# Ties in the gates, key tiles 0 and 1 turned into one tile's two banks, and the last SwiGLU block's two last products exchanged

## The chip, the cores and the metric

The kernel runs on one core of one Trainium2 chip. The metric is the device time of one execution in microseconds (us). A core has five engines with instruction queues of their own: TensorE (PE in the profile, with its weight loads as PEld), VectorE (DVE), ScalarE (ACT), GpSimd (POOL) and SyncE (SP, used here to issue transfers). Each works through its own queue in order and waits for the others by semaphores. An instruction that waits holds up everything behind it in its own queue.

## The reference

One encoder layer over 16 learned meta tokens and 512 tokens, width 1024, in float32:

```python
xn = rmsnorm(h, norm_mix_g)
sb_q, sb_k, sb_v, df_q, df_k, df_v = split(xn @ w_in)
o_sb = stick-breaking attention(sb_q, sb_k, sb_v)            # 8 heads of 128
o_df = differential attention(df_q, df_k, df_v)              # 8 heads, two softmax maps of 64
o_df = rmsnorm(o_df, subln_g) * (1 - lam_init)               # per head
y_sb = o_sb @ w_br_sb
y_df = o_df @ w_br_df
gates = sigmoid(xn @ w_gate + b_gate)                        # two gates of 1024 channels
h = h + (gates[0] * y_sb + gates[1] * y_df) @ w_out
hn = rmsnorm(h, norm_ffn_g)
h = h + (silu(hn @ w_ffn_gate) * (hn @ w_ffn_up)) @ w_ffn_down   # inner width 2816
y = rmsnorm(h, norm_final_g)
```

## The kernel before, in words

Every float32 product is made of three TensorE products of a rounded high half and a low remainder. `split` makes the halves of a weight tile: a ScalarE cast (`wh`, line 78) and a VectorE subtraction (`wl`, line 79). `mm3` (lines 290 to 292) issues the three products, and the third is the one that needs `wl`. The weights arrive in chunks of 512 KB through SP (line 204), are staged, split some chunks ahead of use (`prepare`), and used once. Several large products (keys and values of most heads, the output projection, the SwiGLU block) are made of seven block products instead of eight, from sums of blocks; `c1` to `c4` prepare the weight sums.

The order of the work is only partly written by hand. The program is traced in order, and a planner puts every instruction into its engine's queue: of those that are ready by its own estimate, it takes the one that was traced first. `tc.high_priority(offset=EVAC)` moves an instruction ahead in that ranking, `tc.add_manual_dep` ties an instruction behind another one. The planner's durations are estimates, so the order that it fixes may be wrong for the chip.

The stages that the change touches, in order of time:

- **Attention heads** (eight stick-breaking heads, then eight differential ones). In each, `attn_out` turns the attention blocks (query by key) into key by query with TensorE transposes (line 555), key tile by key tile j = 0, 1, 2. Tile 0 has four blocks (512 columns), tile 1 three, tile 2 two, and one more block (line 557) makes `a_f`. ScalarE copies each turned tile from PSUM as `a_h` (line 559), VectorE makes the remainder `a_l` (line 560), and `weighted` multiplies them with the values (lines 290 to 292, 582, 583). `turn_first` does tiles 0 and 1, `turn_rest` does tile 2. PSUM has eight banks of 512 columns: the pool `ps_z` has two tiles of two banks each (`z_tile`), the pool `ps_mm` four tiles of one bank (`mm_tile`, `tr_tile`). A stick-breaking head takes two z tiles for its turn: tile 0 goes into bank 0 of the first, tile 1 into bank 0 of the second, tile 2 into bank 1 of the first. A differential head takes single banks of `ps_mm`.
- **End of the last differential head.** Its norm (`norm`, lines 769 to 776: Ln and Exp on ScalarE with a VectorE step between it and `o_h`, then `o_l`) is run late, among the gate products. The gates of channel blocks f = 1 and 2 are copied out raw (line 807), and their four sigmoids (line 1053) follow in the trace after all that. Sigmoid is in another function table of ScalarE than Ln and Exp; a change of table is an instruction of its own in the profile (ACT_TABLE_LOAD).
- **Gates and merge** (lines 1105 to 1128). For f in the order 1, 2, 0, 3 to 7: the branch outputs `y_sb` and `y_df`, which were summed up in DRAM, are loaded (line 1065, into memory that the attention pool held before), multiplied by the gates (line 1122: on GpSimd for f < 6, on VectorE after), and added (the merge, line 1126); `merge_sums` splits the result for the output projection. The gates for f = 0 were stored early and come back by a load with a sigmoid behind it (lines 1117, 1118). The last y outputs are added up in DRAM by transfers that GpSimd issues (line 800). Then the residual input is loaded into `hres` by four transfers that GpSimd issues (line 1133); the output projection adds to it (line 1207).
- **SwiGLU block**, 22 blocks f of 128 channels, each in seven block products with `first`, `second`, `third`. `third` ends a block with product a22 into bank e1 and product s4 into bank e3; `second` has copied e1 as `qx` and `qy` (lines 1317, 1322) and added e3 to `qy` (line 1323). The last block is followed by the down projection, whose first weight chunks go into the memory of `hT_l` (the tile `slots`).

Of the kernel before, what the change touches and what calls it, by code (L numbers as in the profile page):

```python
# [41 lines left out]
def block_kernel(ctx: ExitStack, tc: tile.TileContext, x, meta, norm_mix_g, w_in, w_gate, b_gate,  # L42
# [33 lines left out]

    def split(hi, lo, src, lo_eng=None, hi_copy=None):
        cast["last"] = (hi_copy or nc.scalar.copy)(hi, src)  # L78
        (lo_eng or nc.vector).tensor_tensor(lo, src, hi.bitcast(F32), op=ALU.subtract)  # L79

    stream = []

# [133 lines left out]
    def generic(n):  # L216
        wh, wl = parts(n)
        split(wh, wl, staged[n], nc.gpsimd if n < 3 else None)

    K1, K2 = slice(0, 4), slice(4, 8)  # L220

# [9 lines left out]
    def c2(f, g, u, pool, bufs):  # L231
        s = pool.tile([P, KT, P], F32, tag="s21", bufs=bufs, name="s21")
        first = nc.vector.tensor_tensor(s[:, K2], u[:, K1], u[:, K2], op=ALU.add)
        if f in (2, 3):
            behind = mybir.DependencyInfo(mybir.DependencyClass.Sync, mybir.DependencyReason.DATA)
            tc.add_manual_dep(first.ins, cast["hn" if f == 2 else "bf"].ins.name, behind)
        nc.vector.tensor_tensor(s[:, K1], s[:, K2], g[:, K1], op=ALU.add)
        wh, wl = chunk()
        split(wh, wl, s)
        ops[f, "s2"], ops[f, "s1"] = (wh[:, K1], wl[:, K1]), (wh[:, K2], wl[:, K2])  # L240
        ops[f, "s"] = s
# [302 lines left out]
    def attn_out(blocks, d, lo_rows, banks):  # L544

        qn = P - lo_rows
        off = (0, 512, 896)
        a_h = ap_.tile([P, 1152], F32R, tag="a_h", name="a_h")
        a_l = ap_.tile([P, 1152], F32R, tag="a_l", name="a_l")
        a_f = ap_.tile([P, P], F32, tag="a_f", name="a_f")  # L550

        def turn(j, pt):
            n = 512 - j * P
            for t in range(j, NQ):
                nc.tensor.transpose(pt[:, (t - j) * P:(t - j + 1) * P], blocks(t, j * P, (j + 1) * P), ident)  # L555
            if j == 2:
                nc.tensor.transpose(pt[:, 384:512], blocks(3, 3 * P, 4 * P), ident)
            c = slice(off[j], off[j] + n)
            nc.scalar.copy(a_h[:, c], pt[:, 0:n])
            nc.vector.tensor_tensor(a_l[:, c], pt[:, 0:n], a_h[:, c].bitcast(F32), op=ALU.subtract)  # L560

        def turn_first():
            for j, pt in enumerate(banks(2)):
                turn(j, pt)
            for t in range(NQ):
                b = blocks(t, (t + 1) * P - 32 + NM, (t + 1) * P + NM)
                for i in range(qn // 32):
                    nc.vector.transpose(a_s[32 * t:32 * t + 32, t * qn + 32 * i:t * qn + 32 * i + 32],
                                        b[lo_rows + 32 * i:lo_rows + 32 * i + 32])

        def turn_rest():
            p2 = banks(1)[0]
            turn(2, p2)
            nc.scalar.copy(a_f, p2[:, 384:512])

        def weighted():
            vf, vh, vl = d["v"]
            ps = z_tile()[:, 0]
            for j in range(3):
                n = 512 - j * P  # L580
                mm3(ps[:, j * P:512], [(vh[:, j], vl[:, j], a_h[:, off[j]:off[j] + n], a_l[:, off[j]:off[j] + n])], j == 0, False)
            nc.tensor.matmul(ps[:, 3 * P:512], lhsT=vf[:, 0], rhs=a_f, start=False, stop=False)
            nc.tensor.matmul(ps.rearrange("p (t q) -> p t q", q=P)[:, :, lo_rows:P], lhsT=vf[:, 1],
                             rhs=a_s[:, 0:4 * qn], start=False, stop=True)
            return ps

        return turn_first, turn_rest, weighted


# [20 lines left out]
    def sb_head(h, d, o_h, o_l):  # L610
        qh, ql = d["q"]
        kh, kl = d["k"]
        zA, zB = z_tile(), z_tile()

        def score(o, t, k0, k1):
            q = slice(t * P, (t + 1) * P)
            mm3(o, [(qh[:, q], ql[:, q], kh[:, k0:k1], kl[:, k0:k1])])

        score(zA[:, 0, 0:256], 0, 0, 256)
        score(zA[:, 0, 144:416], 1, 0, 272)  # L620
        score(zA[:, 1, 0:416], 2, 0, 416)
        score(zB[:, 0, 0:HL], 3, 0, HL)
        score(zB[:, 1, 0:HL], 3, HL, L)
        res = []
        for z, n in ((zA, 416), (zB, HL)):
            zz = z[:, :, 0:n]
            e = ap_.tile([P, 2, n], F32, tag=("w2" if n == 416 else "w1"), name="e")
            s = ap_.tile([P, 2, n], F32, tag=("w3" if n == 416 else "w0"), name="s")
            nc.scalar.activation(e, zz, AF.Abs)
            nc.scalar.activation(e, e, AF.Exp, scale=-1.0)  # L630
            nc.scalar.activation(e, e, AF.Ln, bias=1.0)
            nc.vector.scalar_tensor_tensor(s, zz, 0.0, e, op0=ALU.max, op1=ALU.add)  # L632
            sf = s.rearrange("p a b -> p (a b)")
            for a, b in (((0, 144), (144, 416), (416, 816)) if n == 416 else ((0, L),)):
                f = sf[:, a:b][:, ::-1]
                nc.vector.tensor_tensor_scan(f, resets[:, L - (b - a):][:, ::-1], f, BIG, op0=ALU.mult, op1=ALU.add)  # L636
            nc.vector.tensor_tensor(s, zz, s, op=ALU.subtract)  # L637
            nc.scalar.activation(s, s, AF.Exp)
            res.append(sf)
        base = ((0, 0), (0, 144), (0, 416), (1, 0))  # L640
        zs = []

        def banks(n):
            if n == 1:
                return [zs[0][:, 1]]
            zs.extend((z_tile(), z_tile()))
            return [z[:, 0] for z in zs]

        t1, t2, av = attn_out(lambda t, k0, k1: res[base[t][0]][:, base[t][1] + k0:base[t][1] + k1], d, 96, banks)
        yield 4 if h + 1 < SEVEN else 5  # L650
        t1()
        yield 1
        t2()
        yield 1
        ps = av()
        nc.scalar.copy(o_h, ps)
        nc.vector.tensor_tensor(o_l, ps, o_h.bitcast(F32), op=ALU.subtract)
# [36 lines left out]
    def df_head(h, d, o_h, o_l):  # L694
# [72 lines left out]
        def norm():  # L767
            pv = tr_tile()
            nc.tensor.matmul(pv, lhsT=ones_r, rhs=sql, start=True, stop=False)
            nc.tensor.matmul(pv, lhsT=ones_r, rhs=sqh, start=False, stop=True)  # L770
            nc.scalar.activation(sq, pv, AF.Ln, bias=eps_c)
            nc.scalar.activation(sq, sq, AF.Exp, scale=-0.5)
            nc.vector.scalar_tensor_tensor(sq, pv, var_max, sq, op0=ALU.is_le, op1=ALU.mult)
            nc.vector.tensor_tensor(of, of, sq, op=ALU.mult)
            nc.scalar.activation(o_h, of, AF.Copy, scale=g_sub)
            nc.vector.scalar_tensor_tensor(o_l, of, g_sub, o_h.bitcast(F32), op0=ALU.mult, op1=ALU.subtract)  # L776
# [273 lines left out]
        for u in units:  # L1050
            u()
    for sg in sg0 + sg1:
        nc.scalar.activation(sg, sg, AF.Sigmoid)
    att.close()


# [54 lines left out]
    for i, f in enumerate(merge_order):  # L1111
# [3 lines left out]
        for br, y in enumerate(ys[i]):  # L1115
            if f == 0:
                nc.sync.dma_start(sg[br], g_part[br])
                nc.scalar.activation(sg[br], sg[br], AF.Sigmoid)
            elif f > 2:
                for u in gate(br, f, sg[br], AF.Sigmoid):  # L1120
                    u()
            (nc.gpsimd if f < 6 else nc.vector).tensor_tensor(sg[br], sg[br], y, op=ALU.mult)
        if f == KT - 1:
            prepare(prep_at["out", "s1", 2])
        m = mf[:, f] if f < 4 else sg[0]
        nc.vector.tensor_tensor(m, sg[0], sg[1], op=ALU.add)
        merge_sums(f, m)
    use_table(LN_EXP)


    hres = xtp.tile([P, NQ, D], F32, tag="y_sb", name="hres")
    for t in range(NQ):
        nc.gpsimd.dma_start(hres[:, t], xv[:, t])
    ssq = [small.tile([P, 2], F32, tag=f"ssq{t}", bufs=2, name="ssq") for t in range(NQ)]

    hT_h, hT_l = (xtp.tile([P, NM + KT * SEQ], F32R, tag=t, name=n)[:, NM:].rearrange("p (k t) -> p k t", t=SEQ)
# [134 lines left out]
    with tc.tile_pool(name="ffn", bufs=1) as fp:  # L1271
# [53 lines left out]

        def third(f, qx, qy):
            e1, e2, e3, sg = bank[f]
            product(f, "a22", tsum["t4"], e1, False)
            with tc.high_priority(offset=EVAC):
                nc.vector.scalar_tensor_tensor(aT[:, f, T1], e1, -1.0, sg[:, T1], op0=ALU.mult, op1=ALU.mult)  # L1330
            product(f, "s4", tsum["b22"], e3, False)
            with tc.high_priority(offset=EVAC):
                nc.vector.tensor_tensor(sg[:, T2], e3, qx, op=ALU.add)
            nc.scalar.activation(sg[:, T2], sg[:, T2], AF.Silu)
            nc.vector.scalar_tensor_tensor(aT[:, f, T2], qy, -1.0, sg[:, T2], op0=ALU.mult, op1=ALU.mult)

        for f in range(2):
            sg = fw.tile([P, SEQ], F32, tag="sg", bufs=2, name="sg")
# [191 lines left out]
```

## Time and profile before

| | |
|---|---|
| times of three runs | 950.56, 948.53 and 2375.36 us, median 950.56 |
| the profiled execution's own time | 949.31 us |
| its span in the profile | 947.5 us |
| TensorE busy | 929.5 us of the span |
| VectorE, ScalarE, GpSimd busy | 733.9, 586.3, 186.8 us |
| mean granted TensorE clock | 0.997 |
| transfers | 158.41 MB |

The profile is of one execution. Its times count from the start of the span. A row of the timeline has the start, the duration, the engine, the line of the kernel, the operation, the tile written and the tiles read (`out<-in`), the shape, and in brackets how long the engine had stood idle and what ended that. A row of the waits has the waiting engine and line, the releaser, the total in us, the number and the longest. A row of the windows has the stretch, its length, busy time (and count) of PE, PEld, DVE, ACT and POOL, the granted clock, the busy share of the DMA engines and GB/s.

### The profile page before, as it was taken

How to read it: one execution, taken by the hardware profiler on the slowest of the kernel's cores; microseconds unless marked ns; L12 is line 12 of the kernel's file. 1: busy time of each engine (PE TensorE's matmuls, PEld its weight loads, DVE VectorE, ACT ScalarE, POOL GpSimd, SP SyncE). 2: the span in 40 equal slices, each digit the busy share in tenths (PEclk: the TensorE clock that was granted, in tenths of full speed). 3: DMA queues.
4: the chain of work that ended last, by engine and by line, in shares of the span. 5: the costliest groups of instructions: out<-in, count | busy, mean ns of one | idle time of the engine just before them, and what ended most of it. 6: DMA issues, size and time to landing. Idle time of an engine off the chain costs nothing.

```text
span 947.5 us, 16049 instructions
## 1 busy us (share of the span) xinstructions
PE 929.5 (98%) x6009; PEld 843.6 (89%) x6010; DVE 733.9 (77%) x1400; ACT 586.3 (62%) x1105; POOL 186.8 (20%) x211
## 2 busy tenths in 40 slices
PE   8999999999999999999999899999999999999997
PEld 5988999898999999999887688899999999978886
DVE  6988878776678766787653578899888888989875
ACT  6665676676656666666774355765555555566654
POOL 3000121222323344344504330001000000000013
PEclk9999999999999999999999999999999999999999
DMA  8525778778767889799958854537743343286642
GB/s 248 143 68 157 176 170 203 168 164 251 192 198 184 196 190 190 162 208 191 198 155 203 262 172 163 144 80 175 158 124 112 93 131 90 68 259 202 198 153 89
DMA packets 155823, 158.41 MB, mean 167 GB/s; under 512 B 6465, under 2 KB 117218, under 8 KB 155746
## 3 DMA queue, kind: packets, MB, share of 16 engines
q1 hardware_dynamic: 132690, 101.61, 35.9%
q0 software_dynamic: 22896, 55.72, 28.8%
q8 instruction: 47, 0.77, 0.3%
q14 instruction: 30, 0.25, 0.1%
q10 hardware_dynamic: 160, 0.07, 0.0%
HBM read 133.64 MB, written 50.86 MB: 195 GB/s over the span
## 4 chain that ended last, share of the span: by engine, by line
PE 76%; DVE 12%; issue 4%; ACT 3%; DMA 3%; POOL 1%; SPq 0%; POOLq 0%; ACTq 0%; DVEq 0%
PE mm L292 17%; PE mm L291 17%; PE mm L290 17%; PE z L290 6%; PE z L291 6%; PE z L292 6%; DVE wl L79 3%; DVE s L636 2%; PE z L705 1%; PE z L704 1%; ACT wh L78 1%; PE tr L555 1%; DMA wsu<-in_w_in_dram 1%; DVE s L637 1%; DVE s L632 1%
## 5 line engine op out<-in xcount | busy, mean ns | idle before, releaser
L292 PE MATMUL mm<-xT_h,wl 128*128 128x264 f32 (+2 forms) x656 | 213.5, 325 | 3.3 <-DVE wl L79 3.3
L291 PE MATMUL mm<-xT_l,wh 128*128 128x264 f32 (+2 forms) x656 | 214.3, 327 | 0.5
L290 PE MATMUL mm<-xT_h,wh 128*128 128x264 f32 (+2 forms) x656 | 214.3, 327 | 0.5 <-ACT xT_h L909 0.5
L79 DVE TENSOR_TENSOR wl<-wst,wh 128x1024 fp32r<-128x1024 f32 (+1 forms) x147 | 166.4, 1136 | 31.1 <-ACT wh L78 30.7
L78 ACT CAST wh<-wst 128x1024 fp32r<-128x1024 f32 (+1 forms) x147 | 141.8, 966 | 76.2 <-PE mm L291 55.2
L292 PEld LDWEIGHTS mm<-xT_h,wl 128*128 128x128 f32 x656 | 124.0, 189 | 13.7 <-DVE wl L79 3.7
L290 PEld LDWEIGHTS mm<-xT_h,wh 128*128 128x128 f32 x656 | 124.0, 189 | 10.4 <-ACT xT_h L909 0.9
L291 PEld LDWEIGHTS mm<-xT_l,wh 128*128 128x128 f32 x656 | 123.8, 189 | 10.4 <-DVE xT_l L910 1.3
L290 PE MATMUL mm<-hT_h,wh 128*128 128x256 f32 x304 | 85.9, 284 | 1.2 <-ACT qx L1317 0.8
L292 PE MATMUL mm<-hT_h,wl 128*128 128x256 f32 x304 | 85.9, 284 | 0.0
L291 PE MATMUL mm<-hT_l,wh 128*128 128x256 f32 x304 | 85.8, 283 | 0.0
L290 PEld LDWEIGHTS mm<-hT_h,wh 128*128 128x128 f32 x304 | 57.9, 191 | 1.8 <-ACT qx L1317 1.2
L292 PEld LDWEIGHTS mm<-hT_h,wl 128*128 128x128 f32 x304 | 58.1, 191 | 0.0
L291 PEld LDWEIGHTS mm<-hT_l,wh 128*128 128x128 f32 x304 | 58.1, 191 | 0.0
L708 DVE CUSTOM_DVE_ANT_0 pr<-z,bias 128x144 f32<-128x144 f32 (+3 forms) x64 | 30.9, 501 | 34.2 <-PE z L705 31.9
L290 PE MATMUL mm<-o_h,wh 128*128 128x512 f32 x128 | 53.2, 415 | 0.1
L291 PE MATMUL z<-wl,da 128*128 128x512 f32 (+1 forms) x132 | 50.4, 382 | 0.6 <-DVE wl L79 0.6
L291 PE MATMUL mm<-o_l,wh 128*128 128x512 f32 x128 | 50.1, 391 | 0.3 <-DVE o_l L776 0.3
L290 PE MATMUL z<-wh,da 128*128 128x512 f32 (+1 forms) x132 | 50.3, 381 | 0.0
L1432 POOL TENSOR_TENSOR outs<-hres,gF 128x512 f32<-128x512 f32 x4 | 6.2, 1548 | 223.6 <-DVE hres L1418 216.8
L292 PE MATMUL z<-wh,da 128*128 128x512 f32 (+1 forms) x132 | 50.2, 380 | 0.0
L292 PE MATMUL mm<-o_h,wl 128*128 128x512 f32 x128 | 50.2, 392 | 0.0
(366 smaller groups left out, 2515.5 us busy)
## 6 DMA issues: line engine op xcount, KB each, us to landing
wst<-in_w_in_dram SPq DMA_DIRECT2D x40, 512.0 KB, 5.9
ds<-in_w_ffn_down_dram POOLq DMA_DIRECT2D x30, 512.0 KB, 6.1
wst<-in_w_ffn_gate_dram SPq DMA_DIRECT2D x22, 512.0 KB, 4.0
wsu<-in_w_ffn_up_dram SPq DMA_DIRECT2D x20, 512.0 KB, 3.8
wst<-in_w_gate_dram SPq DMA_DIRECT2D x16, 512.0 KB, 8.6
y_df<-y_out POOLq DMA_DIRECT2D x32, 256.0 KB, 7.2
slots<-ds SPq DMA_DIRECT2D x13, 512.0 KB, 3.3
os<-in_w_out_dram POOLq DMA_DIRECT2D x12, 512.0 KB, 4.6
```

Of the source, the lines that this page charges most:

```text
L78: cast["last"] = (hi_copy or nc.scalar.copy)(hi, src)
L79: (lo_eng or nc.vector).tensor_tensor(lo, src, hi.bitcast(F32), op=ALU.subtract)
L290: nc.tensor.matmul(ps, lhsT=ah, rhs=bh, start=(start and i == 0), stop=False, skip_group_check=skip)
L291: nc.tensor.matmul(ps, lhsT=ah, rhs=bl, start=False, stop=False, skip_group_check=skip)
L292: nc.tensor.matmul(ps, lhsT=al, rhs=bh, start=False, stop=(stop and i == n - 1), skip_group_check=skip)
L555: nc.tensor.transpose(pt[:, (t - j) * P:(t - j + 1) * P], blocks(t, j * P, (j + 1) * P), ident)
L632: nc.vector.scalar_tensor_tensor(s, zz, 0.0, e, op0=ALU.max, op1=ALU.add)
L636: nc.vector.tensor_tensor_scan(f, resets[:, L - (b - a):][:, ::-1], f, BIG, op0=ALU.mult, op1=ALU.add)
L637: nc.vector.tensor_tensor(s, zz, s, op=ALU.subtract)
L704: nc.tensor.matmul(o, lhsT=q[c][:, qs], rhs=k[c][:, 0, k0:k1], start=True, stop=False)
L705: nc.tensor.matmul(o, lhsT=q[c][:, qs], rhs=k[c][:, 1, k0:k1], start=False, stop=True)
L708: nc.vector.tensor_tensor_reduce(po, zz, bb, scale=1.0, scalar=-3.0e38, op0=ALU.add, op1=ALU.max, accum_out=mx[:, t, c:c + 1])
```

## The change

- `split` also remembers its subtraction, and `generic` the subtraction of the last weight chunk split (`cast["split"]`). A helper `behind` makes the tie that `c2` wrote out before.
- In the heads, both transposes of `turn_first` are traced ahead of both copies. A stick-breaking head takes one z tile for key tiles 0 and 1 (its two banks) and another one for key tile 2.
- The four sigmoids at line 1053 are tied behind the last norm's Exp (`cast["norm"]`).
- For f = 3 to 6, the merge is tied behind the last weight split traced before it.
- The four loads of `hres` are tied behind the last GpSimd multiply (`cast["gated"]`, f = 5).
- In the last SwiGLU block, `third` traces product s4 and what follows it ahead of product a22 and what follows that.

```diff
     def split(hi, lo, src, lo_eng=None, hi_copy=None):
         cast["last"] = (hi_copy or nc.scalar.copy)(hi, src)
-        (lo_eng or nc.vector).tensor_tensor(lo, src, hi.bitcast(F32), op=ALU.subtract)
+        cast["lo"] = (lo_eng or nc.vector).tensor_tensor(lo, src, hi.bitcast(F32), op=ALU.subtract)
+
+    def behind(ins, name):
+        tc.add_manual_dep(ins.ins, cast[name].ins.name,
+                          mybir.DependencyInfo(mybir.DependencyClass.Sync, mybir.DependencyReason.DATA))
...
         split(wh, wl, staged[n], nc.gpsimd if n < 3 else None)
+        cast["split"] = cast["lo"]
...
         def turn(j, pt):
-            n = 512 - j * P
             for t in range(j, NQ):
                 nc.tensor.transpose(pt[:, (t - j) * P:(t - j + 1) * P], blocks(t, j * P, (j + 1) * P), ident)
-            if j == 2:
-                nc.tensor.transpose(pt[:, 384:512], blocks(3, 3 * P, 4 * P), ident)
+
+        def keep(j, pt):
+            n = 512 - j * P
             c = slice(off[j], off[j] + n)
             nc.scalar.copy(a_h[:, c], pt[:, 0:n])
             nc.vector.tensor_tensor(a_l[:, c], pt[:, 0:n], a_h[:, c].bitcast(F32), op=ALU.subtract)
 
         def turn_first():
-            for j, pt in enumerate(banks(2)):
-                turn(j, pt)
+            both = banks(2)
+            for j in range(2):
+                turn(j, both[j])
+            for j in range(2):
+                keep(j, both[j])
...
         def turn_rest():
             p2 = banks(1)[0]
             turn(2, p2)
+            nc.tensor.transpose(p2[:, 384:512], blocks(3, 3 * P, 4 * P), ident)
+            keep(2, p2)
             nc.scalar.copy(a_f, p2[:, 384:512])
...
-        zs = []
-
-        def banks(n):
-            if n == 1:
-                return [zs[0][:, 1]]
-            zs.extend((z_tile(), z_tile()))
-            return [z[:, 0] for z in zs]
-
-        t1, t2, av = attn_out(lambda t, k0, k1: res[base[t][0]][:, base[t][1] + k0:base[t][1] + k1], d, 96, banks)
+        t1, t2, av = attn_out(lambda t, k0, k1: res[base[t][0]][:, base[t][1] + k0:base[t][1] + k1], d, 96,
+                              lambda n: (lambda z: [z[:, i] for i in range(n)])(z_tile()))
...
-            nc.scalar.activation(sq, sq, AF.Exp, scale=-0.5)
+            cast["norm"] = nc.scalar.activation(sq, sq, AF.Exp, scale=-0.5)
...
     for sg in sg0 + sg1:
-        nc.scalar.activation(sg, sg, AF.Sigmoid)
+        behind(nc.scalar.activation(sg, sg, AF.Sigmoid), "norm")
...
-            (nc.gpsimd if f < 6 else nc.vector).tensor_tensor(sg[br], sg[br], y, op=ALU.mult)
+            if f < 6:
+                cast["gated"] = nc.gpsimd.tensor_tensor(sg[br], sg[br], y, op=ALU.mult)
+            else:
+                nc.vector.tensor_tensor(sg[br], sg[br], y, op=ALU.mult)
...
-        nc.vector.tensor_tensor(m, sg[0], sg[1], op=ALU.add)
+        merged = nc.vector.tensor_tensor(m, sg[0], sg[1], op=ALU.add)
+        if 2 < f < KT - 1:
+            behind(merged, "split")
         merge_sums(f, m)
...
     for t in range(NQ):
-        nc.gpsimd.dma_start(hres[:, t], xv[:, t])
+        behind(nc.gpsimd.dma_start(hres[:, t], xv[:, t]), "gated")
...
+            def up():
+                product(f, "a22", tsum["t4"], e1, False)
...
+            def gate_and_up():
+                product(f, "s4", tsum["b22"], e3, False)
...
+            for half in (up, gate_and_up) if f < NFF - 1 else (gate_and_up, up):
+                half()
```

More of the change, by code (lines that the diff above doesn't have):

```diff
@@ L234, in c2 @@
         if f in (2, 3):
-            behind = mybir.DependencyInfo(mybir.DependencyClass.Sync, mybir.DependencyReason.DATA)
-            tc.add_manual_dep(first.ins, cast["hn" if f == 2 else "bf"].ins.name, behind)
+            behind(first, "hn" if f == 2 else "bf")
         nc.vector.tensor_tensor(s[:, K1], s[:, K2], g[:, K1], op=ALU.add)
@@ L1327, in third @@
             e1, e2, e3, sg = bank[f]
[L1328 to L1335, printed above, removed]
+            def up():
+                product(f, "a22", tsum["t4"], e1, False)
+                with tc.high_priority(offset=EVAC):
+                    nc.vector.scalar_tensor_tensor(aT[:, f, T1], e1, -1.0, sg[:, T1], op0=ALU.mult, op1=ALU.mult)
+            def gate_and_up():
+                product(f, "s4", tsum["b22"], e3, False)
+                with tc.high_priority(offset=EVAC):
+                    nc.vector.tensor_tensor(sg[:, T2], e3, qx, op=ALU.add)
+                nc.scalar.activation(sg[:, T2], sg[:, T2], AF.Silu)
+                nc.vector.scalar_tensor_tensor(aT[:, f, T2], qy, -1.0, sg[:, T2], op0=ALU.mult, op1=ALU.mult)
+            for half in (up, gate_and_up) if f < NFF - 1 else (gate_and_up, up):
+                half()
         for f in range(2):
```

## The prediction

> **What bounds the kernel now.** I read the busy times first, then TensorE's (PE's) waits, and then went to each wait with the timeline.
>
> ```profile
> PE 929.5 (98%) x6009; PEld 843.6 (89%) x6010; DVE 733.9 (77%) x1400; ACT 586.3 (62%) x1105; POOL 186.8 (20%) x211
> ...
> PE mm L292 <- DVE wl L79: 3.3, 1, 3.3
> PE z L555 <- DVE a_l L560: 1.5, 2, 1.0
> ...
> 525.00:540.00 15.00, 11.70 (x44) 8.95 (x43) 7.19 (x7) 5.42 (x9) 7.00 (x8) 0.89 0.85 264
> 540.00:815.00 275.00, 274.59 (x2056) 262.12 (x2055) 235.30 (x374) 160.51 (x270) 14.54 (x12) 1.00 0.48 133
> 940.00:948.00 8.00, 0.64 (x6) 0.44 (x4) 2.11 (x8) 2.34 (x6) 0.72 (x1) 0.84 0.34 131
> ```
>
> PE is busy for 929.5 of 947.5 us, so only 18 us are idle, and 7.4 of them are the last stretch, where nothing is left to multiply. No edit adds or removes a product; only PE's few waits can move. The largest lies in the gates (525 to 540): 3.3 us in one piece, and that row alone has a granted clock under 1 in mid-kernel (0.89).
>
> **The gates, step by step.** First the end of the last differential head, where ScalarE (ACT) alternates between Ln/Exp and Sigmoid:
>
> ```profile
> 493.13 0.69 ACT L807 ACTIVATE sg<-mm,pcol 128x512 f32<-128x512 f32 x1 [0.62 <-PE mm L292]
> 493.84 1.28 ACT L772 ACT_TABLE_LOAD   x1
> 495.13 0.63 ACT L772 ACTIVATE sq<-sq 128x512 f32<-128x512 f32 x1
> ...
> 496.73 1.28 ACT L1053 ACT_TABLE_LOAD   x1
> 498.02 0.63 ACT L1053 ACTIVATE sg<-sg 128x512 f32<-128x512 f32 x1
> 498.56 0.71 ACT L775 ACTIVATE o_h<-of,g_sub 128x512 fp32r<-128x512 f32 x1
> ...
> 498.83 0.39 PE L292 MATMUL mm<-o_h,wl 128*128 128x512 f32 x1
> ...
> 500.10 0.50 PE L291 MATMUL mm<-o_l,wh 128*128 128x512 f32 x1 [0.28 <-DVE o_l L776]
> 500.44 0.40 PE L292 MATMUL mm<-o_h,wl 128*128 128x512 f32 x1
> 500.67 0.40 PE L290 MATMUL mm<-o_h,wh 128*128 128x512 f32 x1
> ...
> 500.18 3.93 DMA y_sb<-y_sb
> ```
>
> Two gate sigmoids run before this norm today, so the function tables are swapped for them and swapped back inside the norm. With all four sigmoids tied behind the norm's Exp, the load at 493.84 goes. The gate's copy at 493.13 waits for PE and stays ahead of the Exp, so the Exp moves by that one load: **1.28 us**. The load and the sigmoid between Exp and o_h stay as they are, because that sigmoid still fills the time in which VectorE (DVE) works for o_h. The two sigmoids that come over from earlier (0.63 each) go into ACT's gaps between the y copies. So o_h and o_l end 1.28 us earlier, o_h at 497.99 and o_l, which today lets PE go at 500.10, at about 498.8; PE wants them at 499.06 and 499.29. The three steps from 498.83 to 500.44 take 1.61 us where a step takes 0.23 (500.44 to 500.67): PE gains 0.92 us there. The first loads of y start when o_l is done (500.18), since they reuse the memory of the attention pool: they too come 1.28 us earlier, and with them the chain of POOL multiplies, loads and sigmoids up to this place:
>
> ```profile
> 528.77 0.63 ACT L1118 ACTIVATE sg<-sg 128x512 f32<-128x512 f32 x1 [6.19 <-DMA sg<-g]
> ...
> 529.49 1.28 POOL L1122 TENSOR_TENSOR sg<-sg,y_sb 128x512 f32<-128x512 f32 x1 [7.14 <-ACT sg L1118]
> ...
> 531.34 1.31 POOL L1122 TENSOR_TENSOR sg<-sg,y_df 128x512 f32<-128x512 f32 x1
> 532.57 0.58 POOL L1133 DMA_DIRECT2D hres<-in_x_dram  x1
> 533.17 1.27 POOL L1122 TENSOR_TENSOR sg<-sg,y_sb 128x512 f32<-128x512 f32 x1
> ...
> L1126 DVE TENSOR_TENSOR mf<-sg x4: 677/692/2318, 518.5 to 540.8; 128x512 f32<-128x512 f32 x4
> ...
> 532.68 2.32 DVE L1126 TENSOR_TENSOR mf<-sg 128x512 f32<-128x512 f32 x1 [1.62 <-POOL sg L1122]
> 534.92 1.21 DVE L79 TENSOR_TENSOR wl<-wst,wh 128x1024 fp32r<-128x1024 f32 x1
> ...
> 532.54 0.40 PE L291 MATMUL mm<-xT_l,wh 128*128 128x512 f32 x1
> 536.19 0.80 PE L292 MATMUL mm<-xT_h,wl 128*128 128x512 f32 x1 [3.25 <-DVE wl L79]
> ...
> 539.57 0.40 PE L291 MATMUL mm<-xT_l,wh 128*128 128x512 f32 x1
> ...
> 536.00:537.00 1.00, 0.81 (x2) 0.72 (x3) 0.89 (x3) 0.04 (x1) 0.00 (x0) 0.50 1.14 338
> ```
>
> PE waits for a low half of weights (wl, 534.92), which stands in DVE's order behind the merge of f = 0, which waits for POOL's second multiply. The merge takes 2.32 us, where the median of its four is 0.69: it ends 0.56 us after the POOL multiply beside it. The tie of the hres loads behind f = 5 takes the issues (0.58 the one shown) out from between the multiplies (530.77 to 531.34 and 532.65 to 533.17). New times: multiplies from 528.21 to 529.49, to 530.80 and to about 532.1; the merge ends 0.56 later at 532.7, wl at 533.85 instead of 536.13. That is **2.28 us** earlier for PE, and it holds PE's 0.92 inside it, since wl is still the last to come: PE has run out by 531.7 (532.94 less 1.28) and idles 2.2 us instead of 3.25.
>
> The clock: PE's last work before the wait ends at 532.94, and in the us from 536 the granted clock is 0.50, some 3.0 us later. Eight steps from 536.19 to 539.57 take 3.38 us instead of 1.82. A wait of 2.2 us stays under those 3.0, so **1.56 us** more goes. The Trainium skill (TensorE: Matmul & The Clock Gate, What's actually happening) says that the clock drops after an idle window of about 3.4 us and that the windows run freely; by that figure this 3.25 us wait should not have cost any clock, and its drop would be no work of this wait. The trace has the drop behind 3.0 us of idleness, and I go by the trace.
>
> The merge tie (f = 3 to 6 behind the last weight split) costs nothing: in the order of before, the splits that it names already stand ahead of those merges, on the same engine. If it ever bound, the ScalarE casts of the merged tile and the next gate's tiles would wait behind DVE's merge.
>
> **The hres loads after f = 5.** POOL's last multiply and the first reader:
>
> ```profile
> 555.73 2.27 POOL L1122 TENSOR_TENSOR sg<-sg,y_df 128x512 f32<-128x512 f32 x1
> ...
> 573.70 0.68 DVE L1207 TENSOR_TENSOR hres<-hres,mm 128x512 f32<-128x512 f32 x1
> ...
> DMA to landing us min/median/max: 4.0/5.0/6.5
> ```
>
> Four issues of some 0.58 from 558.0 on end at 560.3; with 6.5 us to landing all are there at 566.8, 6.9 us ahead of the first add. Cost nothing, and on POOL no multiply stands behind them; each us beyond the spare would be a us of DVE, with the weight splits queued behind it.
>
> **Turning key tiles 0 and 1.** In a stick-breaking head the turn of tile 2 goes into the second bank of tile 0's buffer and waits for its reader. With a buffer of its own it no longer does.
>
> ```profile
> 54.99 0.44 PE L555 MATMUL z<-ident,s 128*128 128x128 f32 x2 [1.03 <-DVE a_l L560]
> ...
> 58.09 0.42 DVE L560 TENSOR_TENSOR a_l<-z,a_h 128x256 fp32r<-128x256 f32 x1
> ...
> 58.54 0.27 ACT L574 COPY a_f<-z 128x128 f32<-128x128 f32 x1 [0.26 <-DVE a_l L560]
> ...
> 59.00 0.39 PE L582 MATMUL z<-a_f,vf 128*128 128x128 f32 x2
> ```
>
> In the first head the 1.03 us are mostly not won: DVE is full there and does tile 2's a_l only at 58.09, so a_f ends at 58.81 and PE uses it at 59.00 today. PE can come 0.19 earlier, no more. The other wait of this kind (the row of the waits has two, 1.5 us together) is 0.46 in a later head with room behind it, and stays won. **0.65 us** together; bounds 0 and 1.49. In differential heads the two banks were separate already: nothing.
>
> **The last SwiGLU block.** Product s4 (bank e3) is to run ahead of a22, which frees hT_l, into which the first down weights are loaded:
>
> ```profile
> 833.00 0.42 DVE L1323 TENSOR_TENSOR qy<-z,qy 128x256 f32<-128x256 f32 x1
> ...
> 835.07 1.87 SPq L204 DMA_DIRECT2D slots<-in_w_ffn_down_dram  x4
> ...
> 842.51 0.40 PE L290 MATMUL z<-wh,da 128*128 128x512 f32 x1
> 843.55 0.50 PE L291 MATMUL z<-wl,da 128*128 128x512 f32 x1 [0.65 <-DVE wl L79]
> ```
>
> s4 adds into the bank that qy is read from, and that read ends at 833.42. Today s4 starts right then, with a22 run in the meantime. So putting s4 first can't start it sooner unless DVE is sooner. I take **0**, since a planner that takes whatever is ready will still run a22 in that gap. Bounds: if DVE comes sooner, the wait at 843.55 goes (842.51 to 843.55 is 1.04 for a step of 0.23): minus 0.81. If PE holds still for s4, a22's 1.37 us (12 products of 256 columns) lie behind it: plus 1.37.
>
> **The sum.** 0.65 + 2.28 + 1.56 + 0 = 4.49 us from the profiled execution's 949.31: 944.8. The two ordinary runs shown (948.53 and 950.56) have their middle at 949.55, 0.24 above it: **945.0**. Behind the gates PE is busy for 274.59 of 275 us (540 to 815), so a gain there is carried on.
>
> **Rivals.**
> - *The wait at 536 goes altogether* (0.17). PE would want wl at about 531.5 then (532.54 and one step of 0.23, less the 1.28 by which all ahead of it moves), so wl, done at 536.13 today, has to come 4.6 us earlier: 1.0 from POOL, 3.6 from o_h. That is so if the Exp follows the Ln at once, ahead of the gate copy at 493.13, which starts 2.0 us ahead of today's Exp, and if the y_df loads keep up. All of 3.25, 1.56 and 0.92 goes, and 0.65: 943.2; with the last block's 0.81, 942.4. For it: that copy only waits for PE. Against: it has a raised priority.
> - *The chain of y doesn't move* (0.20), as loads of y_df behind POOL's queue set it and not o_l: then only POOL's 1.0 us is won and PE's 0.92 lengthens the wait to 3.2, with its half clock: 949.55 - 0.65 - 1.0 = 947.9. Or o_l's 1.28 is won, but a POOL multiply falls beside wl and stretches it as it did the merge (by 1.63): 949.55 - 0.65 - 0.65 = 948.3. The Trainium skill (GPSIMD Engine Reference, Key points) has POOL contend with DVE instructions of two SBUF inputs, which wl is. By that rule this is what happens whenever a multiply meets it; the merge of 2.32 us agrees.
> - *Slower: the sigmoid of the stored gates (L1118) one weight earlier in ACT's order* (0.10). It waits for its load until 528.77 and stands ahead of the cast of the weights that PE lacks at 536. If the new order puts it ahead of the weights before those too, they come at 531.7 (sigmoid 528.1, cast 1.05, split 1.22, and 1.28 of POOL beside it). PE wants them at about 526.1 (one product of 24 steps, 5.4 us, before, and 0.92 earlier): 5.6 us of idleness and 1.56 of clock against today's 4.81. 949.55 + 2.35 - 0.92 - 0.65 = 950.3. It decides as soon as it passes that one cast.
> - *The exchange holds PE still* (0.05): 945.0 + 1.37 - 0.81 = 945.6. That the exchange does nothing at all is the forecast itself.
>
> **Chances and range.** Forecast 0.45 (944 to 946.5), the rivals as given. About 2%, 19 us, is what a measurement of this kernel can tell from no change; no case reaches it, and an order reshuffled everywhere is left 0.02 on the slow side and 0.01 on the fast. Range 941.5 (all bounds at their good end: 949.55 less 1.49, 3.25, 1.56, 0.92 and 0.81) to 950.8 (the slow rival, and half a us for the spread of runs).
>
> **What would show it.** Right: no table load at L772, one at L1053; o_h near 497.3 relative to before; no hres issue between POOL multiplies; the wait at L292 near 2.2 us with the clock at 1.00 behind it; no PE wait at L555. Wrong: a wait above 3 us in the gates, a wait of PE at s4 (z from hT), DVE waiting for hres, or new idle rows in stretches that are full now.

## The result, and the profile after

The changed kernel takes **943.89 us** (median of four runs, 943.15 to 945.19; the profiled execution 945.19 with a span of 943.4). The kernel before, on the same chip, takes 949.81 us (median of 948.53, 949.81 and 950.56). Two disturbed runs, one of 2375.36 us here and one of 1309.59 us in experiment 6, are left out of all medians and ratios. The ratio over the runs is 0.9941 (0.9938 by these medians), with a 95% interval of 0.9921 to 0.9961. The forecast was 945.0. A second comparison on another chip gave 942.95 against 948.76: 0.9938 (0.992 to 0.9957). So the gain is 5.8 to 5.9 us by the medians and 4.1 us between the two profiled executions. It is real, and it is less than the 2% that a single measurement tells from no change.

First the busy times of the changed kernel:

```profile
span 943.4 us, 16031 instructions
...
PE 927.4 (98%) x6010; PEld 842.3 (89%) x6010; DVE 731.4 (78%) x1400; ACT 581.6 (62%) x1102; POOL 188.2 (20%) x211
```

PE does the same work in a shorter span. Its busy time fell by 2.1 us (929.5 before), although no product went: matmuls run longer at half clock, and that stretch, worth 1.4 us, is gone. PE's waits after (totals, times, longest):

```profile
PE mm L294 <- ACT qx L1324: 1.5, 2, 0.8
PE mm L296 <- DVE wl L79: 1.5, 1, 1.5
...
PE z L295 <- DVE a_l L564: 0.9, 1, 0.9
PE z L294 <- DVE a_l L564: 0.6, 1, 0.6
...
PE z L294 <- DVE qy L1330: 0.4, 1, 0.4
```

The wait for wl in the gates went from 3.3 to 1.5 us. The two waits at the key tiles' transposes are gone, but two others, 0.9 and 0.6 us, stand at the products that read a_l (lines 294 and 295, the former 290 and 291). A new wait of 0.4 us for qy belongs to the exchange. The windows show the gates and the exchanged block's surroundings:

```profile
525.00:540.00 15.00, 13.55 (x60) 10.91 (x59) 8.63 (x11) 6.74 (x12) 5.98 (x4) 1.00 0.66 177
815.00:830.00 15.00, 13.86 (x112) 13.22 (x112) 13.92 (x23) 7.56 (x14) 0.00 (x0) 1.00 0.31 108
830.00:845.00 15.00, 14.73 (x69) 12.02 (x68) 11.63 (x18) 10.94 (x16) 0.00 (x0) 1.00 0.82 278
```

In 525 to 540 PE executes 60 matmuls where it executed 44, and the granted clock is 1.00 instead of 0.89.

Setting the starts of the same matmul in the two traces side by side gives the account of the profiled pair (after minus before): -0.66 us behind the heads, -1.58 behind the last norm, -1.94 at the last product ahead of the wait in the gates, -3.75 behind it (532.44 where it was 536.19), -5.18 once the half clock of before is over, -4.40 at 819 us (0.7 us lost to a wait for qx whose weights landed later), -4.52 behind the last SwiGLU block, -4.1 at the end.

Now the rows that the prediction spoke of. ACT at the end of the last differential head, after:

```profile
490.67 0.69 ACT L773 ACTIVATE sq<-tr,eps_c 128x512 f32<-128x512 f32 x1 [1.56 <-PE tr L772]
491.39 0.63 ACT L774 ACTIVATE sq<-sq 128x512 f32<-128x512 f32 x1
492.04 1.28 ACT L1055 ACT_TABLE_LOAD   x1
493.33 0.63 ACT L1055 ACTIVATE sg<-sg 128x512 f32<-128x512 f32 x1
493.87 0.67 ACT L809 ACTIVATE sg<-mm,pcol 128x512 f32<-128x512 f32 x1
494.44 0.71 ACT L777 ACTIVATE o_h<-of,g_sub 128x512 fp32r<-128x512 f32 x1
```

The load inside the norm is gone, one is left behind the Exp. But the Exp follows the Ln at once, ahead of the gate copy, which I had said would stay ahead of it. o_h starts 4.1 us earlier (498.56 before). Then POOL's queue, first before, then after:

```profile
501.76 0.86 POOL L800 DMA_DIRECT2D y_df<-y_out  x1 [26.07 <-ACT y_out L796]
504.27 1.28 POOL L1122 TENSOR_TENSOR sg<-sg,y_sb 128x512 f32<-128x512 f32 x1 [1.65 <-DMA y_sb<-y_sb]
505.52 0.85 POOL L800 DMA_DIRECT2D y_df<-y_out  x1
506.10 1.58 POOL L1122 TENSOR_TENSOR sg<-sg,y_sb 128x512 f32<-128x512 f32 x1
507.35 2.95 POOL L800 DMA_DIRECT2D y_df<-y_out  x3
517.20 1.28 POOL L1122 TENSOR_TENSOR sg<-sg,y_df 128x512 f32<-128x512 f32 x1 [6.90 <-DMA y_df<-y_df]
```

```profile
498.91 3.51 POOL L1125 TENSOR_TENSOR sg<-sg,y_sb 128x512 f32<-128x512 f32 x2 [23.89 <-DMA y_sb<-y_sb]
502.37 4.41 POOL L802 DMA_DIRECT2D y_df<-y_out  x5
515.73 1.29 POOL L1125 TENSOR_TENSOR sg<-sg,y_df 128x512 f32<-128x512 f32 x1 [8.96 <-DMA y_df<-y_df]
```

The first y_sb multiply starts 5.4 us earlier, but both now stand ahead of all five transfers that sum y_df up in DRAM. So the first transfer goes out 0.6 us later than before (502.37, 501.76), and the first y_df multiply comes only 1.47 us earlier, when PE itself is 1.58 us ahead at the norm: against PE, the chain gained nothing there. Last, the f = 0 chain that ends PE's wait, after:

```profile
526.48 1.29 POOL L1125 TENSOR_TENSOR sg<-sg,y_sb 128x512 f32<-128x512 f32 x1 [5.60 <-ACT sg L1120]
528.13 1.30 POOL L1125 TENSOR_TENSOR sg<-sg,y_df 128x512 f32<-128x512 f32 x1 [0.37 <-ACT sg L1120]
529.46 0.69 DVE L1131 TENSOR_TENSOR mf<-sg 128x512 f32<-128x512 f32 x1 [1.42 <-POOL sg L1125]
529.65 1.65 POOL L1125 TENSOR_TENSOR sg<-sg,y_sb 128x512 f32<-128x512 f32 x1 [0.22 <-ACT sg L809]
530.07 2.31 DVE L79 TENSOR_TENSOR wl<-wst,wh 128x1024 fp32r<-128x1024 f32 x1
532.44 0.50 PE L296 MATMUL mm<-xT_h,wl 128*128 128x512 f32 x1 [1.45 <-DVE wl L79]
```

No hres issue stands between the multiplies. The merge takes its 0.69 us, but now the next multiply lies beside wl, which takes 2.31 instead of 1.21.

### The profile page after: what moved, and what is told of

Its sections match the earlier page's. It is cut to its first block, busy times and chain, and to the rows that moved or that the text cites. A ratio compares the mean times of both kernels' runs of the same rounds, so it can differ in the third digit from the quotient of the medians.

```text
span 943.4 us, 16031 instructions
## 1 busy us (share of the span) xinstructions
PE 927.4 (98%) x6010; PEld 842.3 (89%) x6010; DVE 731.4 (78%) x1400; ACT 581.6 (62%) x1102; POOL 188.2 (20%) x211
## 4 chain that ended last, share of the span: by engine, by line
PE 80%; DVE 9%; DMA 4%; ACT 3%; issue 3%; POOL 1%; SPq 0%; ACTq 0%; POOLq 0%; DVEq 0%
PE mm L294 19%; PE mm L295 18%; PE mm L296 18%; PE z L294 6%; PE z L295 6%; PE z L296 6%; DVE wl L79 3%; PE z L707 1%; PE z L706 1%; DMA wsu<-in_w_in_dram 1%; PE tr L558 1%; ACT wh L78 1%; PE tr L535 1%; DMA sg<-g 1%; DVE s L645 1%
```

## The experiments

Each kernel is compared with the kernel before on its own chip; the edit is given against the kernel before ("alone") or the changed one ("the whole change without").

**1. Which tie carries the gates?** My sum gave the sigmoid tie 1.28 us and the hres tie 1.0. Three kernels on one chip (before: 949.39): the sigmoid tie alone, the whole change without it, and the whole change without the hres tie.

```diff
 only_sigmoid (before, and)
-        nc.scalar.activation(sg, sg, AF.Sigmoid)
+        behind(nc.scalar.activation(sg, sg, AF.Sigmoid), "norm")
 no_sigmoid (whole change, and)
-        behind(nc.scalar.activation(sg, sg, AF.Sigmoid), "norm")
+        nc.scalar.activation(sg, sg, AF.Sigmoid)
 no_hres (whole change, and)
-        behind(nc.gpsimd.dma_start(hres[:, t], xv[:, t]), "gated")
+        nc.gpsimd.dma_start(hres[:, t], xv[:, t])
```

> The kernel before with the sigmoid tie alone. Theory (this tie carries the gates): the table loads inside the norm go, PE's wait for o_h and o_l goes (0.92), wl is awaited some 1.5 to 1.8 us instead of 3.25 and the clock stays at 1.00, so some 4.6 us less than before, about 945.5, with the hres issues still between POOL's multiplies. Rival (the hres tie carries the wait for wl): wl comes at most 1.3 us earlier, PE still idles about 3 us with the half clock, 1 to 2 us less than before, 948 to 949.

> The changed kernel without the sigmoid tie (turn, hres tie and exchange stay). Theory: the turn's 0.7 us and little else; the wait for wl stays over 2.5 us and PE's wait for o_h is back; 948.5 to 949.5. Rival (hres tie): POOL's multiplies close up, wl comes 1.0 to 1.5 us earlier, the clock no longer drops: 946 to 947.

> The changed kernel without the hres tie; its other queues stay in the same order, POOL's four issues stand between the multiplies again. Theory: the second multiply waits for its sigmoid anyway, so the multiplies move by 0.2 us or less and the wait for wl stays at about 1.5 us: 943.9 to 944.5. Rival (hres tie): 1.0 us or more is lost, wait for wl 2.5 us: 945 to 946.5.

Measured: the sigmoid tie alone 947.54 us, ratio 0.9987 (0.9972 to 1.0003); the whole change without it 943.60, 0.9951 (0.9935 to 0.9968), with a wait for wl of only 0.61 us; without the hres tie 946.78, 0.9975 (0.9961 to 0.9989), with a wait of 2.8 us and half clock behind it. My theory fell: most of the gain stays without the sigmoid tie (0.9951, where the whole change has 0.9941 and 0.9938) and mostly goes without the hres tie. What the sigmoid tie adds to the rest is not told apart from nothing. The timeline of the kernel without the hres tie shows why that tie can be worth more than its 1.0 us:

```profile
524.30 1.28 POOL L1125 TENSOR_TENSOR sg<-sg,y_sb 128x512 f32<-128x512 f32 x1 [5.38 <-ACT sg L1120]
525.73 0.63 ACT L1120 ACTIVATE sg<-sg 128x512 f32<-128x512 f32 x1 [1.21 <-DMA sg<-g]
...
527.00 0.60 POOL L1140 DMA_DIRECT2D hres<-in_x_dram  x1 [1.41 <-DMA y_df<-y_out]
527.60 1.31 POOL L1125 TENSOR_TENSOR sg<-sg,y_df 128x512 f32<-128x512 f32 x1
...
532.45 0.50 PE L296 MATMUL mm<-xT_h,wl 128*128 128x512 f32 x1 [2.82 <-DVE wl L79]
```

The first hres issue does not only take 0.60 us. It waits 1.41 us at the head of POOL's queue until the last transfers out of y_out have landed (the program puts hres into memory of the tag that the y copies used), and the second multiply stands behind it: its sigmoid is done at 526.36, and it starts 1.24 us later. The kernel with the sigmoid tie alone has the same row, in its timeline

```profile
529.08 0.60 POOL L1143 DMA_DIRECT2D hres<-in_x_dram  x1 [0.72 <-DMA y_df<-y_out]
```

In the profile before, this wait could not be seen: there the gates of f = 0 landed late (issued at 521.05, used at 528.77, 7.7 us; after 519.60 and 525.76, 6.2 us), so the first multiply ended only after y_out was free.

**2. The turn alone**, on the same chip.

```diff
 only_turn (before, and)
-            for j, pt in enumerate(banks(2)):
-                turn(j, pt)
+            both = banks(2)
+            for j in range(2):
+                turn(j, both[j])
+            for j in range(2):
+                keep(j, both[j])
...
-            zs.extend((z_tile(), z_tile()))
-            return [z[:, 0] for z in zs]
+                              lambda n: (lambda z: [z[:, i] for i in range(n)])(z_tile()))
```

> The kernel before with the new turn of key tiles 0 and 1 alone. Theory: PE's two waits at the turn go (1.5 us), but the first head gives its 1.0 us back at the products with a_l, so 0.65 us by the end of the stick-breaking heads and 949.5 in all; the gates are as before, a wait of 3.25 us with the half clock. Rival (the whole wait is won): 1.5 us by the end of those heads, 948.7.

Measured: 947.67 us, 0.9988 (0.9969 to 1.0006). The waits at the transposes are gone, and 0.9 and 0.6 us of waits for a_l have come. The order of the queues says why: in six of the later stick-breaking heads the copies of key tile 1 have fallen behind a weight's cast and split. This kernel, too, has the issue that waits (its timeline):

```profile
528.97 0.60 POOL L1138 DMA_DIRECT2D hres<-in_x_dram  x1 [1.22 <-DMA y_df<-y_out]
```

**3. The hres tie alone**, on a second chip (before: 948.72), with the edit of that line only.

```diff
-        nc.gpsimd.dma_start(hres[:, t], xv[:, t])
+        behind(nc.gpsimd.dma_start(hres[:, t], xv[:, t]), "gated")
```

> The kernel before with the tie of the hres loads alone; the queues of PE, DVE and ACT are those of before, and on POOL the four issues stand behind the last multiply. Theory on record (the issues are worth their own 1.0 us, the rest of the gates' gain is the sigmoid tie's): wl comes 1.0 us earlier, so PE waits 2.2 to 2.3 us for it, keeps its clock or not, and the time is 1.0 to 2.6 us under before. Rival from the first four runs (the first issue stands in POOL's queue waiting until the last y_out transfers have landed, since hres takes their memory): 1.3 to 2 us more are taken out, so that PE waits under 1.8 us at L292, the granted clock stays at 1.00, and the time is 2.8 to 4 us under before, most of what the whole change gives, with no sigmoid tie in it.

Measured: 946.73 us, 0.998 (0.9967 to 0.9992), 2.0 us under before. PE's wait came out at 1.78 us, as the new theory had it, but half clock followed, so the time is short of what it expected. Its timeline and its windows:

```profile
528.84 1.28 POOL L1130 TENSOR_TENSOR sg<-sg,y_sb 128x512 f32<-128x512 f32 x1 [5.38 <-ACT sg L1125]
530.14 1.42 POOL L1130 TENSOR_TENSOR sg<-sg,y_df 128x512 f32<-128x512 f32 x1
531.67 1.75 POOL L1130 TENSOR_TENSOR sg<-sg,y_sb 128x512 f32<-128x512 f32 x1
532.21 2.29 DVE L79 TENSOR_TENSOR wl<-wst,wh 128x1024 fp32r<-128x1024 f32 x1
534.56 0.50 PE L296 MATMUL mm<-xT_h,wl 128*128 128x512 f32 x1 [1.78 <-DVE wl L79]
```

```profile
532.49:535.91 3.42, 1.64 (x8) 1.11 (x7) 2.91 (x4) 0.82 (x3) 0.93 (x1) 1.00 0.59 158
535.91:539.32 3.41, 3.41 (x10) 2.65 (x9) 1.72 (x3) 1.36 (x2) 1.73 (x1) 0.50 0.53 150
```

The second multiply can start when the first one is over and its own sigmoid is done. From that moment to the start of the product that waits for wl, all nine layer profiles with the hres tie give 4.38 to 4.45 us (the changed kernel 4.39). The four without it give 5.42 (before) and 5.93, 6.09 and 6.27 (sigmoid alone, without hres, turn alone). The three long ones are those in which the issue waits. So the tie is worth about 1 us in this chain where the wait is hidden, and 1.5 to 1.9 us where it is not.

**4. From which wait on does the clock fall?** This kernel leaves the layer out and measures the clock by itself: bursts of matmuls with pauses between them, which a chain of VectorE operations sets.

```python
for i, n in enumerate(gaps):                      # n = 2 to 10, in four orders
    for k in range(36 + i % 3):
        nc.tensor.matmul(ps, lhsT=w, rhs=rhs[i % 2], start=True, stop=True)
    nc.vector.tensor_tensor(tmp, ps, xs[:, 2, 0:512], op=ALU.add)
    for k in range(n - 2):
        nc.vector.tensor_tensor(tmp, tmp, xs[:, 3, 0:512], op=ALU.max)
    nc.vector.tensor_tensor(rhs[(i + 1) % 2], tmp, xs[:, 1, 512:1024], op=ALU.min)
```

> A kernel that leaves the whole layer out: 36 bursts of 36 to 38 matmuls of 128x512, with pauses between them that a chain of 2 to 10 VectorE operations sets (some 0.6 to 0.7 us each, so pauses of about 1.5 to 7 us), in four orders. It asks from which pause on the granted clock falls to 0.5. Read on record: from about 3.0 us on, and a pause of 2.2 us keeps the clock. Rival from the first four runs, where waits of 2.4, 2.5 and 2.8 us were each followed by half clock and one of 0.6 and one of 1.5 not: the bound lies between 1.5 and 2.4 us. Second rival: it is no bound of the pause but of windows that run on their own, so that one and the same pause drops the clock in some bursts and not in others.

All 55 changes of the clock read after the start lie on one grid of 3.4133 us, within 0.003 us. So the clock is set once per window, and the windows do not care when a pause begins. Cut on that grid, all windows at full clock fall apart cleanly: with up to 1.83 us of idleness the next one is at full clock, from 2.02 us on it is at half. Two pairs of windows of this kernel (here the columns are PE, PEld, DVE and POOL):

```profile
342.96:346.38 3.42, 1.58 (x7) 1.32 (x8) 1.72 (x3) 0.00 (x0) 1.00 0.02 5
346.38:349.79 3.41, 3.41 (x17) 2.83 (x16) 0.00 (x0) 0.00 (x0) 1.00 0.00 0
...
428.30:431.71 3.41, 1.39 (x6) 1.17 (x7) 1.90 (x3) 0.00 (x0) 1.00 0.00 0
431.71:435.12 3.41, 3.41 (x10) 2.63 (x9) 0.00 (x0) 0.00 (x0) 0.50 0.00 0
```

PE was busy for 1.58 and for 1.39 us of the first window of each pair; only behind the second is the clock at 0.50. So a pause seems to be judged by its larger piece in one window. The four pauses of 2.2 us were cut in two each time and cost nothing; every pause of 3.0 us or more cost half clock. By this kernel alone, a bound for the whole pause between 2.24 us (kept) and 2.96 us (lost) would do as well. The layer rules it out: the kernel with the hres tie alone lost its clock behind a wait of 1.78 us that lay in one window, shorter than the cut pauses of 2.2 us that kept it. So the first reading (from 3.0 us) and the rival (a bound for the pause) give way to the second rival, the windows. In the layer the windows at whose end the clock fell in the gates held 2.97 us of idleness (before), 2.49 (sigmoid alone), 2.41 (turn alone), 1.90 (without hres) and 1.78 (hres alone). The changed kernel, with 1.45 in one window, kept it, and so did the run without the sigmoid tie with 0.61. The windows of the changed kernel on its own grid:

```profile
529.52:532.93 3.41, 1.96 (x9) 1.33 (x8) 3.38 (x4) 0.46 (x2) 1.65 (x1) 1.00 0.47 128
532.93:536.34 3.41, 3.41 (x17) 2.80 (x16) 1.90 (x3) 1.94 (x3) 1.11 (x1) 1.00 0.69 207
```

The Trainium skill (TensorE: Matmul & The Clock Gate, What's actually happening) gives the window as 3413 ns and free-running, which the grid here confirms. It calls for an idle window; here a window that was a little over half idle sufficed.

**5. Can the chain be made shorter still?** On the second chip: the two early y_sb multiplies on DVE, and with that the copies of key tiles 0 and 1 raised in rank.

```diff
 ysb12_dve (whole change, and)
-            if f < 6:
+            if br == 0 and f in (1, 2):
+                nc.vector.tensor_tensor(sg[br], sg[br], y, op=ALU.mult)
+            elif f < 6:
 best (ysb12_dve, and)
+            with tc.high_priority(offset=250):
                 for j in range(2):
                     keep(j, both[j])
```

> The whole change, and the two y_sb multiplies of f = 1 and 2, which stand ahead of the y_df transfers in POOL's queue (3.51 us each, from 498.9 to 502.4 and on), done by DVE instead. Theory (POOL's queue order ahead of the y_df transfers is what keeps the sigmoid tie's 1.28 us from the chain of y): the y_df transfers go out 2 to 4 us earlier, the f = 0 sigmoid and multiplies come 1.3 to 3 us earlier, the wait of 1.5 us for wl goes to under 0.5, and the time is 1 to 1.5 us under the whole change (942.4 to 942.9 where that has 943.9). Rival (the chain is set by the y copies and the landing of the sums in DRAM): the load of y_df lands within 0.5 us of 511.3 as now, and the time is that of the whole change or up to 1 us above it, as DVE has 1.4 us more to do.

> As the run with the two multiplies on DVE, and the copies of key tiles 0 and 1 raised in rank so that a_h and a_l of tile 1 no longer stand behind a weight's cast and split. Theory (the turn's gain in the heads was given back by these two places, 0.9 and 0.6 us of PE waits): the two waits of PE for a_l go, heads end 1 to 1.5 us earlier, and the time is 1 us or more under the run without it: 941 to 942.5. Rival: the raised copies push weight splits back, and PE waits for wl in the heads instead: same time, or up to 1.5 us more.

(The expectation misreads the row of the two multiplies: 3.51 us is the sum of both.) Measured: 943.46 us, 0.9949 (0.993 to 0.9969), and 944.0, 0.9956 (0.9939 to 0.9973). POOL of the first of the two:

```profile
500.31 0.86 POOL L802 DMA_DIRECT2D y_df<-y_out  x1 [25.18 <-ACT y_out L798]
...
505.12 1.75 POOL L802 DMA_DIRECT2D y_df<-y_out  x2 [1.22 <-ACT y_out L798]
514.34 1.28 POOL L1127 TENSOR_TENSOR sg<-sg,y_df 128x512 f32<-128x512 f32 x1 [7.47 <-PE mm L295]
```

The first transfer goes out 2.1 us earlier than in the changed kernel, but the last issues end at 506.9 (506.8 there): they wait for the y copies, no longer for POOL. The first y_df multiply comes 1.39 us earlier and wl's wait falls to 0.4 us, and still the ratio is no better than the whole change's. With the raised copies the stick-breaking heads end no earlier (0.62 us ahead of the profile before, 0.54 without them), and each differential head then loses some 0.27 us. The expected gains did not show.

**6. The rest on one chip** (before: 948.76): the whole change again, without the exchange, without the turn, and the last version with the copies raised in the stick-breaking heads only.

```diff
 no_exchange (whole change, and)
-            for half in (up, gate_and_up) if f < NFF - 1 else (gate_and_up, up):
+            for half in (up, gate_and_up):
 best2 (best, and)
-            with tc.high_priority(offset=250):
+            with tc.high_priority(offset=250 if lo_rows == 96 else 0):
```

The kernel without the turn takes the edit of experiment 2 back.

> The whole change once more, on the chip of the three runs that follow, so that they can be set against it. Expected 943.9 us, with a wait for wl of about 1.5 us. The clock: the probe kernel's windows of 3.413 us say that half clock follows a window with 1.8 us or more of idleness, so it must stay at 1.00 here unless the wait comes out at 1.8 or more.

> The whole change with product s4 of the last SwiGLU block behind a22 again. The sum on record: no difference. By the two traces: the wait of PE for qy (0.39 us, 0.26 of it lost) goes and the wait at the first down product (0.38 gained) comes back, so 0.1 us slower than the whole change and within the spread of runs. Rival (the exchange is what gains after the gates): 0.5 to 0.8 slower, with a wait of 0.65 for wl at the first down product.

> The whole change with the old turn of the key tiles. The sum on record: 0.65 us slower than the whole change. Rival by the queue orders and the run with the turn alone (the casts of tile 1 fall behind a weight's cast and split in six heads, and PE waits 0.9 and 0.6 us for a_l): what the turn gains is given back, so the same time within 0.3 us, with the two waits at the transposes back (1.0 and 0.5) and no wait for a_l at the values' product.

> The whole change, with the two y_sb multiplies of f = 1 and 2 on DVE, and the copies of key tiles 0 and 1 raised in rank in the stick-breaking heads only (where they were raised in all heads, each differential head lost 0.27 us, 2.1 in all). Theory: the stick-breaking heads end 1 to 1.4 us before those of the whole change, the differential heads lose nothing, wl's wait is under 0.5: 941.0 to 942.5, faster than the whole change by 1.5 to 2.5. Rival: loads that land at other times (the s wait for wsu near 150 us, qx near 815) take the gain back, and it is within 0.5 us of the whole change.

Measured: the whole change 942.95 us (0.9938, 0.992 to 0.9957), without the exchange 942.73 (0.9937, 0.992 to 0.9955), without the turn 944.42 (0.9956, 0.994 to 0.9972), the last version 942.56 (0.994, 0.9921 to 0.9959). The exchange is worth nothing that can be measured. Its waits in the kernel without it:

```profile
PE z L295 <- DVE wl L79: 0.5, 1, 0.5
...
PE z L294 <- DVE qy L1330: 0.2, 1, 0.2
```

PE waits less for qy and more for the first down weights, as expected. The turn's 1.5 us between medians lies above the rival's 0.3 and the sum's 0.65, but the intervals overlap, so its size stays open. The traces point to a gain above the sum: the seven profiles with the turn (raised copies left aside) end the heads 0.29 to 2.06 us ahead of the profile before, the three others without it 0.22 to 0.70 us behind it. The waits of the kernel without the turn

```profile
PE mm L294 <- ACT qq L449: 1.5, 1, 1.5
...
PE z L558 <- DVE a_l L564: 1.2, 2, 1.0
```

show the old wait at the transposes back, and a wait for qq near 151 us (1.5 and 1.6 us in some kernels, 0.2 in the changed one's first profile). It goes along with the landing of a small load that DVE awaits near 140 us (lam, line 839 of the changed kernel): where DVE stands 2.5 to 3.1 us for it, PE waits 1.5 to 1.6 us for qq; where DVE stands 1.2 us or less, 0.2 us or not at all. No edit touched that load. The last version has the shortest profiled span of all, 938.9 us, but its median is 0.4 us from the whole change: not shown to be faster. No version beats the changed kernel by more than the spread of runs.

## Why the prediction was right, point by point

The total was right and the range held the time, but steps inside were wrong, with errors of opposite sign, so that the closeness of the total is partly luck. Behind the heads, the product that waits for wl came 3.09 us earlier in the profiled pair (3.75 less the heads' 0.66), not 2.28. That is 0.79 from the chain of y (forecast 1.28), 1.03 from the hres tie (forecast 1.0), and 1.27 because the stored gates landed sooner after their issue, which the sum did not have and no run shows to be an effect of the change.

- **Table load and norm: right in size, wrong in place.** The load went and PE gained exactly the 0.92 us in the norm (-0.66 to -1.58). The step "the gate's copy stays ahead of the Exp" failed: the Exp follows the Ln, so o_h came 4.1 us earlier, the condition of the first rival. The rival's second condition, that the y_df loads keep up, was not met. Of the signs given in advance, o_h near 497.3 and a wait near 2.2 us did not come.
- **"o_l's 1.28 us is carried through the chain of y": the step that failed.** POOL took the early y loads first and put two multiplies, 3.51 us together, ahead of the y_df transfers. With those two on DVE (experiment 5) the first y_df multiply came 1.39 us earlier, while PE was 0.14 us later behind the norm, so that order is what held the chain back. Less the heads, 0.79 us of the 1.28 arrived, no more than PE itself gained at the norm. The sigmoid tie alone gives 0.9987 with 1 inside its interval.
- **The hres issues at 1.0 us: right for this pair, too small for others.** I priced them as issue time only, because in that one profile the issue did not wait. In three other profiles it waits 0.72 to 1.41 us, and the tie is worth 1.5 to 1.9 us. In the profiled pair it gave 1.03 us (5.42 to 4.39), and the sooner landing of the stored gates made up for the failed step.
- **POOL beside wl:** the merge was freed, but wl was stretched to 2.31 us, as the second rival had said, 1.1 us that my sum did not have; the merge's stretch, 1.63 us, went in exchange. The Trainium skill's rule quoted there (GPSIMD Engine Reference, Key points) agrees with this row.
- **The clock: right in the result (1.43 us won for a forecast 1.56), wrong in the rule.** "A wait of 2.2 us stays under those 3.0" is not how it goes: 2.2 us within one window would have dropped the clock. It was kept because the wait came out at 1.45 us. The 2.2 itself was a slip: it lets PE run out 1.28 us earlier, where the prediction's own gain at the norm was 0.92, so by its numbers the wait was 1.9 us.
- **Turn:** 0.66 for a forecast 0.65 in the profiled pair, which is partly luck: the second profile of the same kernel ends its heads 2.06 us ahead of before. Both old waits are gone, and two new ones, 1.5 us together, stand in their place.
- **Exchange:** 0 forecast; 0.26 lost at qy and 0.38 won at the first down weight, and no difference in time without it. The 0.38 us wait of PE at s4 is one of the signs of being wrong that the prediction named.
- **Merge tie: nothing, as said.** In the traces DVE does the gates in the same order with it (the changed kernel) and without it (before, hres alone); no run leaves it out alone. **hres late: nothing, as said.** DVE does not wait for it. **The slower rival did not arise:** the stored gates' sigmoids keep their place in ACT's order, next ahead of the same cast.
- **Not in the sum:** 0.7 us lost to the wait for qx at 815. The gain by the medians is some 1.7 us more than by the profiled pair; the second profile of the changed kernel (941.2, against the same 947.5) agrees with the medians. That before was profiled in an execution in which the hres issue did not wait points the same way, but is not shown to be the cause. One profile of before is not all of them: of its 31 executions on the chip of experiment 1, the 8 with a mean granted clock of 0.998 or 0.999 took 945.63 to 948.54 us, the 9 with 0.994 took 949.59 to 951.00.
- **A small slip:** the idle time at the end was put at 7.4 us; the span ends at 947.5, so it is 6.9.

## What to carry to other kernels

Before pricing a transfer issue at its issue time, ask whose memory it writes: an issue that waits for a buffer blocks everything behind it on its engine, and one profile can hide that wait. Moving work earlier helps a chain only if the queue of the next engine keeps the chain's own work in front. And a wait of PE costs half clock by how much of one fixed window it fills, so shortening it below that share wins twice.

## What the runs showed of the hardware that was not expected

- The granted clock changes on a grid of 3.4133 us that runs by itself. At full clock, a window with 2.02 us or more of PE idleness was followed by one at half clock in every case of the pure test, one with up to 1.83 never. In the layer 1.78 us lost the clock (hres alone), while 1.82 in the last stretch of the kernel with the turn alone (937.37 to 940.78) and 1.45 in the changed kernel did not. The bound lies near 1.8 us, a little over half the window; these traces do not give it more closely.
- A window at half clock was followed by full clock with up to 0.28 us of idleness in it (before, 535.91 to 539.32), and by another half one from 0.82 us on (the pure test).
- A DVE operation on two SBUF operands took 1.1 to 1.6 us longer beside a POOL multiply: wl 2.29 to 2.32 us instead of 1.21, the merge 2.32 instead of 0.69.
- A transfer issued by POOL stood 0.72, 1.22 and 1.41 us at the head of POOL's queue until other transfers had left the memory that it writes, with the multiplies of the critical chain behind it.
